# A four-mixer network on one core: beginning one output projection with its attention half, and splitting two mixers' weights ahead of time

## The chip, the cores and the metric

The kernel runs on one core of a Trainium2 chip. The metric is the device time of one execution in microseconds (us); less is better. In the traces PE is TensorE, DVE is VectorE, ACT is ScalarE, POOL is GpSimd and SP is SyncE, which here only issues transfers.

## What is computed

A sequence of 512 tokens with 1024 channels, in float32, goes through six stages. Each is a sandwich: normalize, transform, normalize, add to the input.

```python
# block one: h = rms_norm(x, pre); x = x + rms_norm(mixer(h), post)
E1: even_mixer    retention + stick-breaking attention, concatenated, @ w_out
O1: odd_mixer     gated linear recurrence + LRU, concatenated, @ w_out
# block two: x = x + rmsnorm(fn(rmsnorm(x, g_pre)), g_post)
def even_mixer_2(t, ...):                       # E2, the third mixer
    proj = t @ w_in
    y_a = diff_attention(proj[..., :3 * DIFF_WIDTH], ...)   # 4 heads, 512 channels out
    y_b = conformer_conv(proj[..., 3 * DIFF_WIDTH:], ...)   # gated 31-tap causal conv, layernorm, silu
    return jnp.concatenate([y_a, y_b], axis=-1) @ w_out
F0: swiglu(t, w_gate, w_up, w_down)             # hidden width 2816
O2: odd_mixer_2   s5_ssm (256 channels) + mla_attention (6 heads), concatenated, @ w_out
F1: swiglu
```

In `diff_attention` each head's output is the difference of two softmax attentions, and the 128 channels of each head are then divided by their root mean square. In `conformer_conv` the 512 convolved channels of a token go through one layernorm, so that its statistics need all 31 taps of all four channel tiles.

## The kernel before

Tokens lie in four blocks of 128 (`NB = 4`); matrices are cut into 128x128 tiles. To keep float32 accuracy, every large product is made of three matmuls (`mm3`): each operand is split into a high part `h` (a rounded copy) and a low part `l = x - h`, and h·h, h·l and l·h are summed in PSUM. So every weight piece of 128x1024 values has to be split before TensorE can use it. `wload` does that: SP loads the raw piece into one of three `wr` buffers, ACT copies it to `wh` (line 132), DVE subtracts to get `wl` (line 115). `wh` and `wl` have five buffers each. For an output projection some pieces go to larger `wb` tiles (`big=True`), which come from the pool of 14 tiles of 4x512 that also holds activations (`A4`).

`projT` projects with the channels on the partitions, one piece per 128 output channels. `projS` projects with the tokens on the partitions: its four pieces are all needed for each of the four token blocks, so all four stay in their buffers until the last block.

`outp` is the output projection and the two normalizations behind it. The input channels come as pieces in the order `order`. The first `nK - tail` pieces are multiplied into all four token blocks; then, block by block, the last `tail` pieces, so that a block can be normalized while the next is multiplied. Its sums lie in all eight PSUM banks (PP, ZZ, ZO, WW for the four blocks).

The third mixer, `even2`, first projects the convolution's two halves (`e2t`); the 4 x 30 taps (`taps`, line 750, on DVE) have the low priority `prio(-1500)`, so DVE does them when nothing else is ready. Then q, k and v are projected, and four heads go through `scores` (scores, softmax of two score matrices, difference, transposes) and `av_` (times v). The end of the stage, and the order of the output projection, are:

```python
        scores(3)
        av_(1)
        av_(2)
        stats()      # transpose ycv (PE), sums and squares (ACT): needs all taps
        av_(3)
        norm()       # layernorm: rstd and scaling (DVE)
        silu()       # transpose back (PE), Silu (ACT), split: channels 512..1023
        heads()      # over_rms (DVE), transpose (PE), split: channels 0..511
        self.order = [4, 5, 6, 7, 0, 1, 2, 3]
```

The instructions are placed on the five engines' queues when the kernel is built: among those that are ready by the planner's own estimate of times, the one with the highest priority is next (by default program order; `prio(1200)` puts one 1200 instructions further up). On the chip each queue then runs strictly in that order, and waits at its head. Buffers, PSUM banks included, are given out in the same planning, when the first instruction that writes one is placed.

Of the kernel before, what the change touches and what calls it, by code (L numbers as in the profile page):

```python
# [8 lines left out]
F32 = mybir.dt.float32  # L9
F32R = mybir.dt.float32r  # L10
# [7 lines left out]
P = 128  # L18
S = 512
NB = 4  # L20
# [30 lines left out]
class Net:  # L51
    def __init__(self, ctx, tc, A, out):
        self.tc, self.nc, self.A, self.out = tc, tc.nc, A, out
        pool = lambda name, **k: ctx.enter_context(tc.tile_pool(name=name, **k))
        self.cst_p = pool("cst", bufs=1)
        self.w_p = pool("w", bufs=5)
        self.a_p = pool("a", bufs=14)
        self.u_p = pool("u", bufs=13)
        self.s_p = pool("s", bufs=40)
        self.ps = pool("ps", bufs=1, space=PSUM)  # L60
        self.d_p = pool("dram", bufs=1, space=bass.MemoryType.DRAM)

        self.banks = {"P": 2, "Z": 3, "W": 2, "O": 1}
        self.xdram = [self.d_p.tile([P, NB, 2, 512], F32, name=f"xd{i}") for i in range(2)]
        self.xn = 0
        self.gates = []
        self.n = 0
        nc = self.nc
        self.cst = self.cst_p.tile([P, C_N], F32, name="cst")
        nc.gpsimd.dma_start(self.cst[:, :P], A["cst"][:, :P])  # L70
        self.vec = self.cst_p.tile([P, V_N], F32, name="vec")
        self.ident = self.cst[:, C_ID : C_ID + P]
        self.xsrc = A["x"].rearrange("(b p) d -> p b d", p=P)
        self.k = self.cst_p.tile([P, 8], F32, name="k")
        for i, v in enumerate((EPS, 0.0, 1.0, HALF_PI)):
            nc.vector.memset(self.k[:, i : i + 1], v)
        with self.prio(9000):
            nc.scalar.activation(self.k[:, 5:6], self.k[:, 2:3], AF.Sqrt)
        self.ones = self.cst_p.tile([P, P], F32, name="ones")
        nc.vector.memset(self.ones, 1.0)  # L80
        self.eps, self.zero, self.one, self.hpi = (self.k[:, i : i + 1] for i in range(4))
# [36 lines left out]
        self.nc.scalar.copy(h, src)  # L118
        self.lo(l, src, h)

    def wload(self, name, i, cols, big=False, pool=False):
        nc = self.nc
        with self.prio(1200):
            raw = self.w_p.tile([P, 1024], F32, tag="wr", bufs=3, name=self.nm("wr"))[:, :cols]
            nc.sync.dma_start(raw, self.A[name][i])
            if big:
                h, l = (t.rearrange("p a d -> p (a d)") for t in (lambda w: (w[:, 0:2], w[:, 2:4]))(self.A4(F32R, "wb")))
            else:
                h = self.w_p.tile([P, 1024], F32R, tag="wh", name=self.nm("wh"))[:, :cols]
                l = self.w_p.tile([P, 1024], F32R, tag="wl", name=self.nm("wl"))[:, :cols]  # L130
        with self.prio(9000 if self.gates else 1200):
            c = nc.scalar.copy(h, raw)  # L132
            if pool:
                s = nc.gpsimd.tensor_tensor(l, raw, h.bitcast(F32), ALU.subtract)
            else:
                s = self.lo(l, raw, h)
        if self.gates:
            for r, g in zip((c, s), self.gates.pop(0)):
                self.hold(r, g)
        return h, l  # L140

    def mm3(self, out, a, b, first, last, hold=None):
# [129 lines left out]
    def xb(self, b):  # L272
        return self.x[b // 2][:, 2 * (b % 2) : 2 * (b % 2) + 2]

    def outp(self, name, order, lhs, post, pre, tail=7, last=False, nbig=4, in_turn=False):

        nc = self.nc
        yb = [[self.bank(t, "y") for t in tags] for tags in ("PP", "ZZ", "ZO", "WW")]
        nK = len(order)
        gate = max(0, nK - tail - 3)  # L280
        first = []
# [2 lines left out]
        def mm(n, w, b):  # L284
            k = order[n]
            h, l = lhs(k)
            sl = slice(b * P, b * P + P)
            for j in range(2):
# [2 lines left out]
                prev[b] = r  # L291
                if n == gate and not first:
                    first.append(r)

        for n in range(nK - tail):
            w = self.wload(name, order[n], 1024)
            for b in range(NB):
                mm(n, w, b)
        ws = [self.wload(name, order[n], 1024, big=n - nK + tail < nbig) for n in range(nK - tail, nK)]
        with self.prio(100):  # L300
            self.load_x(first[0])
# [8 lines left out]
        for b in range(NB):  # L310
            if in_turn and b > 1:
                held[b, 0] = held[b, 1] = prev[b - 1]
            for n in range(nK - tail, nK):
                mm(n, ws[n - nK + tail], b)
            with self.prio(6000):
# [15 lines left out]
                    self.prenorm(b, prew)  # L331
            if not last:
                nc.scalar.dma_start(dst[:, b], self.xb(b))
        if not last:
            self.xsrc = dst.rearrange("p b a d -> p b (a d)")

# [376 lines left out]
    def even2(self):  # L713
        nc = self.nc
# [134 lines left out]
        scores(3)  # L849
        av_(1)  # L850
        av_(2)
        stats()
        av_(3)
        norm()
        silu()
        heads()
        self.order = [4, 5, 6, 7, 0, 1, 2, 3]


    def exp_tiny(self, dst, x, t, n):  # L860
# [349 lines left out]
def net(ctx, tc, A, out, phases="E1 O1 E2 F0 O2 F1"):  # L1210
    n = Net(ctx, tc, A, out)
    ph = phases.split()
# [4 lines left out]
        n.s5_setup()  # L1217
    for i, p in enumerate(ph):
        lhs = n.mix
        if p == "E1":  # L1220
            n.even1()
        elif p == "O1":
# [5 lines left out]
        else:  # L1228
            n.ffn(p.lower() + "gu")
            lhs = n.lhs  # L1230
            if p == "F0" and "O2" in ph:
                n.s5_setup()
        last = i == len(ph) - 1
        n.outp(wout[p], n.order, lhs, 6 + pres[p], None if last else pres[ph[i + 1]], last=last, in_turn=p == "O2")

# [154 lines left out]
```

## Time and profile before

| | |
|---|---|
| median of three runs | 1719.47 us (1714.02 to 1721.96) |
| the profiled execution, whole | 1708.09 us |
| the profiled execution, first to last instruction (span) | 1706.3 us |
| TensorE busy | 1657.1 us, 97% of the span |
| VectorE busy | 964.3 us, 57% |
| ScalarE busy | 669.6 us, 39% |
| mean granted TensorE clock | 0.987 |

Read it so: TensorE is busy nearly all the time, so what a change can win lies in the few stretches where it is not, or where its clock is granted below 1. All times inside the trace count from the start of the span. E1 takes about the first 241 us with its output projection, O1 goes to about 530, E2 to 759, F0 to 1127, O2 to about 1340 and F1 to the end.

### The profile page before, as it was taken

What the parts mean: (1) busy time and instruction counts of PE and PEld (TensorE: products, weight loads), DVE (VectorE), ACT (ScalarE), POOL (GpSimd) and SP (SyncE); (2) the same over time, 40 slices, a digit from 0 to 9 for tenths busy, and PEclk for the clock granted to TensorE, in tenths of its full rate; (3) what the DMA queues carried; (4) which work ended last, traced back from release to release, by engine and by line L of the source; (5) the groups of instructions that cost most, each with busy time, mean ns of one, the idle gap of its engine ahead of it and who ended that gap; (6) DMA issues with size and microseconds to landing.
All of it is one profiled execution on the core that took longest, in us unless ns stands there. A gap on an engine that the chain in (4) does not pass through costs nothing. (4 is left out here: it accounts for less than half of the span.)

```text
span 1706.3 us, 20536 instructions
## 1 busy us (share of the span) xinstructions
PE 1657.1 (97%) x8008; PEld 1318.5 (77%) x8008; DVE 964.3 (57%) x1824; ACT 669.6 (39%) x1174; POOL 2.0 (0%) x8
## 2 busy tenths in 40 slices
PE   8999999999999998699999999999999999999998
PEld 8657788988789875588888888886447988888886
DVE  7564456765676998763222278468695622224332
ACT  5554234214545246543222244344456422224231
POOL 0000000000000000000000000000000000000000
PEclk8999999999999999799999999999999999999999
DMA  5212243202153220152223235432005323222341
GB/s 204 84 38 74 80 179 117 72 29 99 62 198 115 74 84 1 65 195 101 98 99 99 99 118 196 170 126 78 25 25 197 112 99 99 99 98 89 97 161 50
DMA packets 50241, 175.06 MB, mean 103 GB/s; under 512 B 5584, under 2 KB 6096, under 8 KB 50016
## 3 DMA queue, kind: packets, MB, share of 16 engines
q1 hardware_dynamic: 40896, 142.20, 24.6%
q10 hardware_dynamic: 9216, 31.48, 4.9%
q8 instruction: 63, 1.03, 0.3%
q14 instruction: 34, 0.28, 0.1%
q0 software_dynamic: 32, 0.07, 0.0%
HBM read 156.95 MB, written 16.78 MB: 102 GB/s over the span
## 5 line engine op out<-in xcount | busy, mean ns | idle before, releaser
L115 DVE TENSOR_TENSOR wl<-wr,wh 128x1024 fp32r<-128x1024 f32 (+2 forms) x224 | 271.3, 1213 | 350.4 <-ACT wh L132 335.4
L132 ACT CAST wh<-wr 128x1024 fp32r<-128x1024 f32 (+2 forms) x224 | 233.0, 1042 | 534.8 <-PE pp L147 409.8
L147 PE MATMUL pp<-xl,wh 128*128 128x512 f32 (+1 forms) x1184 | 428.1, 362 | 0.2 <-DVE xl L115 0.2
L144 PE MATMUL pp<-xh,wh 128*128 128x512 f32 (+1 forms) x1184 | 425.2, 361 | 1.2 <-ACT xh L234 1.2
L148 PE MATMUL pp<-xh,wl 128*128 128x512 f32 (+1 forms) x1184 | 425.3, 360 | 0.0
L144 PEld LDWEIGHTS pp<-xh,wh 128*128 128x128 f32 x1184 | 223.6, 190 | 36.1 <-ACT xh L234 2.5
L147 PEld LDWEIGHTS pp<-xl,wh 128*128 128x128 f32 x1184 | 224.4, 190 | 34.0 <-DVE xl L115 1.2
L148 PEld LDWEIGHTS pp<-xh,wl 128*128 128x128 f32 x1184 | 224.4, 190 | 33.7 <-issue 2.3
L147 PE MATMUL pp<-wl,xh 128*128 128x512 f32 (+1 forms) x320 | 126.9, 396 | 0.0
L148 PE MATMUL pp<-wh,xl 128*128 128x512 f32 (+1 forms) x320 | 125.9, 394 | 0.0
L144 PE MATMUL pp<-wh,xh 128*128 128x512 f32 (+1 forms) x320 | 125.9, 393 | 0.0
L144 PE MATMUL y<-wh,ah 128*128 128x512 f32 x288 | 112.5, 390 | 0.0
L147 PE MATMUL y<-wl,ah 128*128 128x512 f32 x288 | 112.3, 390 | 0.0
L148 PE MATMUL y<-wh,al 128*128 128x512 f32 x288 | 112.2, 389 | 0.0
L1189 DVE TENSOR_TENSOR act<-g,pp 128x512 f32<-128x512 f32 x44 | 30.2, 687 | 132.9 <-PE pp L148 131.5
L750 DVE SCALAR_TENSOR_TENSOR ycv<-up,vec,ycv 128x512 f32<-128x512 f32 x120 | 84.4, 740 | 0.4
L144 PEld LDWEIGHTS pp<-wh,xh 128*128 128x128 f32 x320 | 60.2, 188 | 13.9 <-issue 2.6
L147 PEld LDWEIGHTS pp<-wl,xh 128*128 128x128 f32 x320 | 60.2, 188 | 12.9 <-issue 2.4
L148 PEld LDWEIGHTS pp<-wh,xl 128*128 128x128 f32 x320 | 60.3, 188 | 11.1 <-issue 0.6
L321 DVE TENSOR_TENSOR yn<-y,nw 128x512 f32<-128x512 f32 x48 | 31.8, 685 | 58.0 <-ACT yn L319 52.2
L144 PEld LDWEIGHTS y<-wh,ah 128*128 128x128 f32 x288 | 54.1, 188 | 11.5 <-issue 0.4
L148 PEld LDWEIGHTS y<-wh,al 128*128 128x128 f32 x288 | 54.1, 188 | 11.1
(373 smaller groups left out, 2314.0 us busy)
## 6 DMA issues: line engine op xcount, KB each, us to landing
wr<-in_f0gu SPq DMA_DIRECT2D x44, 512.0 KB, 3.3
wr<-in_f1gu SPq DMA_DIRECT2D x44, 512.0 KB, 3.3
wr<-in_f0d SPq DMA_DIRECT2D x22, 512.0 KB, 3.4
wr<-in_f1d SPq DMA_DIRECT2D x22, 512.0 KB, 3.3
xd<-x ACTq DMA_DIRECT2D x20, 512.0 KB, 2.7
x<-xd ACTq DMA_DIRECT2D x20, 512.0 KB, 6.7
wr<-in_o1t SPq DMA_DIRECT2D x16, 512.0 KB, 3.3
nw<-in_nw ACTq DMA_DIRECT2D x12, 512.0 KB, 9.5
```

Source lines behind the costliest of these rows:

```text
L115: return self.nc.vector.tensor_tensor(l, src, h.bitcast(F32), ALU.subtract)
L132: c = nc.scalar.copy(h, raw)
L144: r = mm(out, lhsT=a[0], rhs=b[0], start=first, stop=False)
L147: mm(out, lhsT=a[0], rhs=b[1], start=False, stop=False)
L148: return mm(out, lhsT=a[1], rhs=b[0], start=False, stop=last)
L321: nc.vector.tensor_tensor(yn[j], yb[b][j], postw[j], ALU.mult)
L750: V.scalar_tensor_tensor(y, up[:, j : j + 512], self.v("dw", 4 * j + t), y, ALU.mult, ALU.add)
L1189: nc.vector.tensor_tensor(act[k // 4][:, k % 4], g, ps, ALU.mult)
```

## The change

Two edits in the same step.

1. In E2 the order of the output projection becomes 0 to 7, attention half first, and `stats`, `norm` and `silu` are handed to `outp` as `mid`. `outp` now has `tail=4`: it multiplies the four attention pieces into token blocks 0, 1 and 2, then issues `mid`, then goes on block by block with the four convolution pieces; block 3, whose two banks (WW) `mid` uses for its transposes, gets its attention pieces just before its convolution pieces.
2. During E1 and O1, at every second weight load outside an output projection, one piece of E2's weights is loaded and split (`keep_ahead`), and both halves are stored to DRAM by two transfers from POOL's queue. E1 and O1 have 52 such loads, so 26 of E2's 28 pieces are kept (all but the last two of `e2out`). During F0, with 44 loads, all 19 listed pieces of O2 are kept in the same way (all O2 weights but `o2glu`). When E2 and O2 ask for a kept piece, `wload` loads its two halves straight into `wh` and `wl` (or `wb`), with two transfers from SP and no work for ACT or DVE.

```diff
-    def wload(self, name, i, cols, big=False, pool=False):
-        nc = self.nc
+    def plan(self, pieces, every):
+
+        self.ahead, self.every, self.nw = pieces, every, 0
+
+    def keep_ahead(self):
+        nc = self.nc
+        name, i, cols = self.ahead.pop(0)
+        t = self.d_p.tile([P, 2, cols], F32, name=f"kp_{name}_{i}")
+        for j, s in enumerate(self.wload(name, i, cols, keep=True)):
+            nc.gpsimd.dma_start(t[:, j], s.bitcast(F32))
+        self.kept[name, i] = t
+
+    def wload(self, name, i, cols, big=False, pool=False, keep=False):
+        nc = self.nc
+        if (name, i) in self.kept:
+            t = self.kept[name, i]
+            with self.prio(1200):
+                if big:
+                    h, l = (t.rearrange("p a d -> p (a d)") for t in (lambda w: (w[:, 0:2], w[:, 2:4]))(self.A4(F32R, "wb")))
+                else:
+                    h = self.w_p.tile([P, 1024], F32R, tag="wh", name=self.nm("wh"))[:, :cols]
+                    l = self.w_p.tile([P, 1024], F32R, tag="wl", name=self.nm("wl"))[:, :cols]
+                nc.sync.dma_start(h.bitcast(F32), t[:, 0])
+                nc.sync.dma_start(l.bitcast(F32), t[:, 1])
+            return h, l
...
+        if self.ahead and not keep:
+            self.nw += 1
+            if self.nw % self.every == 0:
+                self.keep_ahead()
         return h, l
...
-    def outp(self, name, order, lhs, post, pre, tail=7, last=False, nbig=4, in_turn=False):
+    def outp(self, name, order, lhs, post, pre, tail=7, last=False, nbig=4, in_turn=False, mid=None):
...
+        ahead, self.ahead = self.ahead, []
...
+        early = []
 
         for n in range(nK - tail):
-            w = self.wload(name, order[n], 1024)
-            for b in range(NB):
-                mm(n, w, b)
+            early.append(self.wload(name, order[n], 1024))
+            for b in range(NB - 1 if mid else NB):
+                mm(n, early[n], b)
+        if mid:
+            mid()
...
+            if mid and b == NB - 1:
+                for n in range(nK - tail):
+                    mm(n, early[n], b)
             for n in range(nK - tail, nK):
                 mm(n, ws[n - nK + tail], b)
...
+        self.ahead = ahead
...
         av_(1)
         av_(2)
-        stats()
         av_(3)
-        norm()
-        silu()
         heads()
-        self.order = [4, 5, 6, 7, 0, 1, 2, 3]
+        self.order = list(range(8))
+
+        def mid():
+            stats()
+            norm()
+            silu()
+
+        self.mid = mid
...
+        if p == "E1" and "E2" in ph:
+            n.plan([("e2t", i, 1024) for i in range(8)] + [(f"e2{z}", i, 1024) for z in "qkv" for i in range(4)]
+                   + [("e2out", i, 1024) for i in range(8)], 2)
+        if p == "F0" and "O2" in ph:
+            n.plan([("o2t", i, 1024) for i in range(2)] + [("o2s", i, 896) for i in range(4)]
+                   + [("o2kv", 0, 768), ("o2q", 0, 768), ("o2q", 1, 768), ("o2q", 2, 768), ("o2kv", 1, 768)]
+                   + [("o2out", i, 1024) for i in (2, 3, 4, 5, 6, 7, 0, 1)], 2)
...
+        n.outp(wout[p], n.order, lhs, 6 + pres[p], None if last else pres[ph[i + 1]], last=last, in_turn=p == "O2",
+               **(dict(tail=4, mid=n.mid) if p == "E2" else {}))
```

## Rows read from the trace of the kernel before

**Rows 1.** The page's busy times: us, share of the span, instructions.

```profile
PE 1657.1 (97%) x8008; PEld 1318.5 (77%) x8008; DVE 964.3 (57%) x1824; ACT 669.6 (39%) x1174; POOL 2.0 (0%) x8
```

**Rows 2.** By stage: length; PE, PEld, DVE, ACT, POOL busy; clock; DMA share; GB/s.

```profile
0.00:488.00 488.00, 478.52 (x2512) 383.26 (x2513) 299.88 (x692) 208.07 (x357) 1.39 (x7) 0.99 0.27 95
548.00:621.00 73.00, 73.00 (x345) 59.28 (x344) 72.82 (x125) 23.64 (x31) 0.00 (x0) 1.00 0.26 87
621.00:655.50 34.50, 34.31 (x145) 22.62 (x145) 30.11 (x91) 20.27 (x54) 0.00 (x0) 1.00 0.13 46
655.50:688.40 32.90, 27.45 (x140) 18.57 (x138) 27.72 (x85) 19.60 (x56) 0.00 (x0) 0.90 0.00 1
688.40:708.80 20.40, 6.20 (x26) 4.63 (x27) 14.22 (x44) 9.94 (x24) 0.00 (x0) 0.55 0.00 0
708.80:759.20 50.40, 48.65 (x226) 39.97 (x225) 31.33 (x46) 27.44 (x48) 0.00 (x0) 0.98 0.49 178
860.00:880.00 20.00, 20.00 (x90) 16.57 (x89) 6.28 (x6) 5.20 (x6) 0.00 (x0) 1.00 0.27 94
1170.00:1290.00 120.00, 113.81 (x393) 57.79 (x393) 97.94 (x206) 61.71 (x143) 0.00 (x0) 0.99 0.11 37
```

**Rows 3.** The hole in slices of 3 us, same columns.

```profile
689.00:692.00 3.00, 0.00 (x0) 0.00 (x0) 2.89 (x5) 0.42 (x1) 0.00 (x0) 0.77 0.00 0
698.00:701.00 3.00, 1.11 (x6) 0.71 (x4) 0.31 (x2) 3.00 (x11) 0.00 (x0) 0.50 0.00 0
713.00:716.00 3.00, 3.00 (x19) 2.53 (x18) 2.82 (x4) 3.00 (x4) 0.00 (x0) 1.00 0.00 0
```

**Rows 4.** The convolution's tile ycv alone: PE, PEld, DVE busy by stretch.

```profile
548.00:621.00 73.00, 0.00 (x0) 0.00 (x0) 52.22 (x77) 1.00 0.26 87
621.00:696.00 75.00, 1.77 (x7) 1.27 (x8) 33.80 (x47) 0.92 0.06 22
```

**Rows 5.** Weight splits: line 115 in three stretches, then line 132's group.

```profile
L115 DVE TENSOR_TENSOR wl<-wr,wh x13: 1215/1218/1224, 549.1 to 619.8; 128x1024 fp32r<-128x1024 f32 x13
...
L115 DVE TENSOR_TENSOR wl<-wr,wh x1: 1209/1209/1209, 622.7 to 622.7; 128x1024 fp32r<-128x1024 f32 x1
...
L115 DVE TENSOR_TENSOR wl<-wr,wh x10: 684/959/1225, 1128.8 to 1184.1; 128x768 fp32r<-128x768 f32 x5, 128x896 fp32r<-128x896 f32 x3, 128x512 fp32r<-128x512 f32 x1, 128x1024 fp32r<-128x1024 f32 x1
...
L132 ACT CAST wh<-wr 128x1024 fp32r<-128x1024 f32 (+2 forms) x224 | 233.0, 1042 | 534.8 <-PE pp L147 409.8
```

**Rows 6.** Timeline 688 to 712: start, duration, work, count, idle before and releaser.

```profile
688.35 0.60 ACT L369 ACTIVATE sq<-po 128x512 f32<-128x512 f32 x1 [1.80 <-PE po L359]
...
688.98 0.69 DVE L371 TENSOR_REDUCE hs<-sq 128x4 f32<-128x512 f32 x1 [1.84 <-ACT sq L369]
689.58 6.25 DVE L750 SCALAR_TENSOR_TENSOR ycv<-up,vec,ycv 128x512 f32<-128x512 f32 x8
...
695.89 0.69 PE L202 MATMUL pt<-cst,ycv 128*128 128x128 f32 x2 [7.58 <-DVE ycv L750]
...
702.15 0.17 DVE L193 TENSOR_SCALAR h<-hs 128x16 f32<-128x16 f32 x1
...
705.94 0.17 DVE L198 SCALAR_TENSOR_TENSOR r<-t,r 128x16 f32<-128x16 f32 x1
706.15 2.50 DVE L382 TENSOR_TENSOR on<-on,r 128x512 f32<-128x512 f32 x4
...
708.85 0.78 PE L144 MATMUL y<-wh,mh 128*128 128x512 f32 x1
...
711.99 1.37 ACT L841 ACTIVATE mh<-pt,lqt 128x512 fp32r<-128x512 f32 x2 [0.74 <-PE pt L202]
```

**Rows 7.** Transfers: issues with KB and us to landing; DMA at 731 to 734.

```profile
xd<-x ACTq DMA_DIRECT2D x20, 512.0 KB, 2.7
...
cst<-in_cst POOLq DMA_DIRECT2D x1, 64.0 KB, 6.3
...
731.00:734.00 3.00, 3.00 (x15) 2.49 (x14) 0.00 (x0) 2.38 (x4) 0.00 (x0) 1.00 1.02 410
```

More of the change, by code (lines that the diff above doesn't have):

```diff
@@ L66, in __init__ @@
         self.gates = []
+        self.kept, self.ahead, self.every, self.nw = {}, [], 0, 0
         self.n = 0
@@ L1233, in net @@
         last = i == len(ph) - 1
-        n.outp(wout[p], n.order, lhs, 6 + pres[p], None if last else pres[ph[i + 1]], last=last, in_turn=p == "O2")
+        n.outp(wout[p], n.order, lhs, 6 + pres[p], None if last else pres[ph[i + 1]], last=last, in_turn=p == "O2",
+               **(dict(tail=4, mid=n.mid) if p == "E2" else {}))
 def _tables(np):
```

## The prediction

> **What bounds the kernel now.** I read the busy times first: TensorE is busy 97% of the span, 1657.1 of 1706.3 us [rows 1]. So only about 49 us can be won at all, plus what is lost to a low clock, and the question is where these lie. The second view, busy time by stage, answers that [rows 2]. Of the first 488 us (E1 and O1) TensorE is idle 9.5. In F0 it is full, 90 matmuls in 20 us, which gives 0.222 us per matmul of 512 columns at full clock. The largest loss is the end of E2. From 655.5 to 688.4 it idles 5.45 us at a mean clock of 0.90, from 688.4 to 708.8 it works only 6.2 of 20.4 us, at 0.55. Together that is 19.65 us of idling. The third view cuts this hole into slices [rows 3]: nothing runs from 689 to 692, the clock is 0.50 from 698 to 701 (1.2 GHz of 2.4), and back at 1.00 by 713.
>
> The fourth view, the timeline [rows 6], says why. At 688.98 the last head is reduced; then DVE has eight taps left, and TensorE waits 7.58 us for them, until 695.89. What follows is a chain over three engines: statistics, layernorm, transposes, Silu, split. It lets the first matmul of the output projection start at 708.85. The attention heads, whose sums of squares were ready at 689.7, wait behind that: their own normalization begins at 702.15, because the convolution half comes first.
>
> Why are the taps late? DVE is busy 72.82 of 73.00 us from 548 to 621 [rows 2]. In that stretch it made 77 taps (52.22 us) [rows 4] and 13 weight splits of 1.22 us [rows 5]; 47 taps were left for the attention, where DVE is again busy 30.11 of 34.5 and 27.72 of 32.9 us. So in E2 every weight split pushes taps back, and the last tap sets the end. That is unlike the rest of the program, where TensorE is the bound.
>
> **Part one: splits leave E2.** Thirteen splits before 621 and one just after leave DVE: 14 x 1.22 = 17.1 us. A tap costs 52.22/77 = 0.68 us while DVE does little else, so 25 more taps fit before 623 or so, and 22 of the 47 remain. DVE has them to do in the 67 us of attention in which it did 39, so I expect the last tap near 660, not at 695.8. Then statistics, layernorm and Silu of the convolution (16 + 16 transposes, 16 ACT instructions) can run in gaps of the attention or just behind it. Their 28 us of cover is what hides them; with the taps still late they cost the chain of now, 695.9 to 708.8, which part two covers.
>
> With some 15 us of taps (22 x 0.68) gone from the stretch 655.5 to 688.4, softmax steps wait less for DVE. At most its idle time and half of what its clock lost can come back, 5.45 + 1.6 = 7 us; the least is nothing, since the statistics move in. I take 3: the last head ends near 685.4.
>
> **Part two: attention half first.** What now precedes the first matmul of the projection is the heads' chain. Its links have rows [rows 6]: square 0.60 and reduction up to 689.67, so 1.3 from 688.35; the 16-wide reciprocal root from 702.15 to 706.11, of which 1.9 belongs to layernorm scaling between, so 2.1; scaling 2.50; transposes and ACT's rounded copy of one head, 1.4 (0.69 of it ACT). That is 7.3, and the first matmul starts near 692.8 instead of 708.85: **16 us earlier**. TensorE is idle meanwhile but for transposes, so I count the low clock at the start of the projection once again, as it is now (0.55 before, 1.00 only by 713 [rows 2, 3]), and keep its whole length of 50.4 us. Inside it, 3 blocks x 4 pieces x 2 x 3 = 72 matmuls, 16 us at 0.222, run before the first convolution piece is needed. So even with the last tap at 695.8 the 13 us chain behind it is nearly covered: the two parts win the same hole, not two.
>
> Block 3 now has 48 matmuls at the end, 10.7 us, blocks 0 to 2 have 24, 5.3 us each, where each had 42; DVE needs some 6 us for a block's normalizations, and can catch up during block 3. Cost: 0, with -2 to +3 in the range.
>
> **Part three: loading instead of splitting in E2 and O2.** A kept piece is 1 MB instead of 0.5, and its transfer can begin only when a `wh` buffer is free, where before the raw piece was waiting in `wr` and needed 1.04 + 1.22 us. At the 410 GB/s of the busiest slice [rows 7] a piece takes 2.6 us. Between q, k and v four pieces follow four that free their buffers in steps of 1.3 us (6 matmuls), so the third and fourth come about 1 us late each time. I take 1.5 us in all; nothing if scores fill the gap, 5 at most. SP's queue holds only loads, so behind a waiting one stand the next pieces and no computation.
>
> In O2, 9 of 10 splits between 1126 and 1184 leave DVE, about 9 us [rows 5], as do 4 to 8 of `o2out` at its end. From 1170 to 1290 TensorE idles 6.2 of 120 us and is otherwise in float32 matmuls [rows 2]: it is nearly the bound, so I take 3 us of gain, with bounds 0 and 9.
>
> **Part four: what is added.** E1 and O1 get 26 splits: 27 us of ACT, 32 of DVE, against 280 and 188 us of idle time there [rows 2]. F0 gets 19, with DVE at 6.28 of 20. 45 pieces are stored by 90 transfers of at most 0.5 MB and read back. In F0 two loads, one more load and two stores per 11 us make 2.6 MB, 240 GB/s, under the 410 seen. The cover is TensorE's own stream; I take 2 us, mostly at the crowded start and in E1's attention.
>
> **The sum.** -16 + 1.5 - 3 + 2 = -15.5. The profiled execution takes 1708.09 us, 1.8 more than its span, so it would take 1692.6, 0.9% less. The median of the runs shown is 1719.47, 0.67% above that execution; the same share off gives 1704.
>
> **Rivals.** *The stores hold the buffers.* Each kept piece occupies one of five `wh` and `wl` buffers until its stores land, and ACT and DVE run in order: a split for a buffer not yet free blocks softmax, evacuation and all else behind it. For: POOL's one transfer took 6.3 us for 64 KB, while a store of 512 KB from ACT's queue took 2.7 [rows 7]; E1 and O1 hold four pieces at a time in seven projections. Against: a group of four lasts 22 us, long enough for a store of 6, and DVE is 61% busy there. The rival cancels the gain at 17.5/26 = 0.7 us of TensorE idle per kept piece in E1 and O1; at 1.2 us it gives +13, 1732 scaled. The Trainium skill, SBUF — State Buffer, section "SBUF: two separate sides", says that a transfer from POOL's queue cannot get its descriptors while DVE runs certain instructions that take both port pairs, so that it looks blocked. By that rule the landing grows with DVE's load; no row here has such a store under a busy DVE.
>
> *The hole only changes its owner.* The heads' chain leaves TensorE idle as the taps did; if the last head still ends at 688.4, DVE mixes taps into the chain (1 tap per link, 5 x 0.68), and loads come late by 5, the gain is 15.5 - 3 - 3.4 - 3.5 - 1 = 4.6 us: 1715, within half a percent, which is about what a measurement of this kernel can tell from no change. For it speaks that the planner placed taps between softmax steps before.
>
> *O2 gives as much as it could.* With 9 us there instead of 3, and 4 more from the attention of E2, it is -25.5: 1694. For it: DVE is at 82% from 1170 to 1290; against: TensorE at 95%.
>
> *The splits leave, yet DVE ends as late*, if taps keep their late places. Then only the reordering works, first matmul near 697 with taps mixed in, and about 10 us are won: 1709.
>
> **How the numbers follow.** Forecast (1704) 0.45, taps late (1709) 0.12, O2 in full (1694) 0.13, changed owner (1715) 0.17, stores (1732) 0.13. Faster by over 0.5% (below 1710.9): most of the first three, 0.66; within: 0.20; slower by over 0.5%: 0.14. The range from 1692 to 1723 leaves out most of the stores' rival and the best of O2; the likeliest case alone has 1698 to 1710.
>
> **What would show it.** Part one: the last tap before 670, no split by line 115 between 548 and 620. Part two: the first matmul of the third output projection near 693, some 7 us behind the last head, and the projection's end near 743 instead of 759. Part three: TensorE waits of about 1 us on loads of `wh` between q, k and v. Part four: E1 and O1 end within 2 us of now. Wrong would be: the start of E2 later by more than 5 us, ACT or DVE waiting on POOL's stores, or idle time of more than 10 us left between the last head and the projection.

## The result: 3% slower, and the profile after

The changed kernel takes 1773.91 us (median of 4 runs, 1767.66 to 1778.81) against 1720.72 us of the kernel before beside it (1714.02 to 1728.97): a ratio of 1.0305, 95% interval 1.0248 to 1.0362. The forecast was 1704 us. The profiled execution of the changed kernel spans 1776.6 us, 70.3 more than the one before.

Busy times of the page, to be read against [rows 1]:

```profile
PE 1691.9 (95%) x8008; PEld 1335.9 (75%) x8008; DVE 966.5 (54%) x1824; ACT 670.3 (38%) x1174; POOL 50.6 (3%) x98
```

TensorE executes as many matmuls as before, is busy 34.8 us longer and idle 35.5 us longer. So half of the loss is waiting, and half is the same work at a lower clock (a mean of 0.969 instead of 0.987). The profiled execution of before (1708.09 us) is shorter than all four timed beside the change, and that of the changed kernel (1778.81) is the longest of its four. So what is 70.3 us between the two profiles is 53.2 us between the medians, and the differences by stage below are 17 us too large in all.

The stages, cut in each trace at the start of the first and the end of the last matmul of each output projection (us; before, E1 ends at 289.7 with its projection, and the 241 given ahead of the prediction is about the end of its mixer):

| stage | before | after | difference |
|---|---|---|---|
| E1 mixer, projection | 242.6, 47.1 | 268.4, 47.0 | +25.7, 0 |
| O1 mixer, projection | 182.5, 52.0 | 202.4, 57.3 | +19.9, +5.3 |
| E2 mixer, projection | 184.6, 50.6 | 170.4, 62.1 | -14.3, +11.5 |
| F0 mixer, projection | 244.1, 123.6 | 258.4, 123.7 | +14.4, 0 |
| O2 mixer, projection | 152.1, 57.3 | 160.8, 58.3 | +8.7, +1.1 |
| F1 to the end | 369.8 | 367.8 | -2.0 |

E2's mixer gives most of what was hoped for. E1 and O1, which only prepare it, lose 51 us; E2's projection and F0's mixer lose 26.

**Where E1 and O1 lose.** Busy times by stretch (columns as in [rows 2]): E1's and O1's mixers of the changed kernel, then of the kernel before.

```profile
0.00:268.35 268.35, 245.23 (x1168) 182.40 (x1169) 156.65 (x392) 126.91 (x221) 16.36 (x35) 0.94 0.50 169
...
315.38:517.77 202.39, 188.16 (x1057) 158.79 (x1056) 129.61 (x259) 79.01 (x114) 12.18 (x22) 0.97 0.46 158
```

```profile
0.00:242.60 242.60, 233.37 (x1168) 176.83 (x1169) 140.04 (x378) 112.81 (x207) 1.39 (x7) 0.98 0.28 97
...
289.70:472.20 182.50, 182.31 (x1056) 154.90 (x1056) 121.02 (x257) 67.06 (x102) 0.00 (x0) 1.00 0.21 74
```

In E1 TensorE idles 23.1 us instead of 9.2, and the same 1168 matmuls take 11.9 us longer at a mean clock of 0.94 instead of 0.98. DVE gets 17 us of work and ACT 14 and both stay far from full, so neither has become the bound. What they do is wait. The view of waits of the changed kernel, 0 to 575 us (sum, times, longest), first ACT and then DVE:

```profile
ACT wh L157 <- DMA kp_e2v<-wh: 10.5, 2, 6.1
ACT wh L157 <- DMA kp_e2t<-wh: 6.2, 2, 4.1
```

```profile
DVE wl L117 <- DMA kp_e2out<-wl: 11.1, 4, 3.8
DVE wl L117 <- DMA kp_e2k<-wl: 9.5, 2, 6.1
DVE wl L117 <- DMA kp_e2t<-wl: 9.1, 2, 6.3
```

With the groups not shown, ACT stands 30.4 us and DVE 38.2 us in front of a split (lines 157 and 117, formerly 132 and 115), because the buffer it is to fill is still being stored. The timeline shows what one such wait does (five answers: POOL, DVE, SP, ACT, PE):

```profile
31.20 0.53 POOL L132 DMA_DIRECT2D kp_e2t<-wl  x1 [0.73 <-DVE lqt L756]
...
37.74 1.22 DVE L117 TENSOR_TENSOR wl<-wr,wh 128x1024 fp32r<-128x1024 f32 x1 [2.81 <-DMA kp_e2t<-wl]
...
39.00 2.46 SPq L150 DMA_DIRECT2D wr<-in_e1sv  x2
...
43.13 1.05 ACT L157 CAST wh<-wr 128x1024 fp32r<-128x1024 f32 x1 [4.02 <-DMA wr<-in_e1sv]
...
47.37 0.76 PE L176 MATMUL pp<-wl,xh 128*128 128x512 f32 x1 [2.63 <-DVE wl L117]
```

DVE has split a kept piece, and POOL issues the store of its low half at 31.20. The very next split on DVE is given the same buffer: it stands at the head of the queue from 34.93, 3.7 us behind the issue, and waits 2.81 us more for the landing. This split frees a raw buffer only at 38.96, so SP issues the next load of E1's own weights at 39.00; ACT waits 4.02 us for that piece, its low half is begun at 46.09, and TensorE idles 2.63 us. That loads wait for splits is nothing new (50 of SP's loads did so up to 524 us of before, 66 up to 575 us here); what is new is that the splits wait for stores, and a late split is a late load. This is the one place where TensorE's idle time ends with a weight split itself. The rest of its 41.8 us up to the end of O1 (9.6 before) ends with other work of DVE and ACT, whose queues hold the waiting splits; that each of these gaps goes back to a held buffer is argued, not followed one by one.

**Where E2 and F0 lose.** The timeline of the changed kernel around the third projection, which answers to [rows 6]:

```profile
738.56 0.69 DVE L409 TENSOR_REDUCE hs<-sq 128x4 f32<-128x512 f32 x1 [3.83 <-ACT sq L407]
...
742.49 2.41 PE L231 MATMUL pt<-cst,on 128*128 128x128 f32 x8 [4.60 <-DVE on L420]
745.46 0.80 PE L173 MATMUL y<-wh,mh 128*128 128x512 f32 x1 [0.56 <-ACT mh L879]
...
765.20 1.03 PE L231 MATMUL pt<-cst,ycv 128*128 128x128 f32 x8
...
773.96 1.97 PE L231 MATMUL pt<-cst,yS 128*128 128x128 f32 x8 [6.15 <-DVE yS L859]
...
778.96 0.79 PE L173 MATMUL y<-wh,mh 128*128 128x512 f32 x1 [0.41 <-ACT m L868]
```

The last head is reduced at 739.25 and the first matmul follows 6.2 us later. But the convolution's transposes start only at 765.20, behind all 72 early matmuls, although its last tap was done at 709.2:

```profile
L788 DVE SCALAR_TENSOR_TENSOR ycv<-up,vec,ycv x120: 673/745/753, 597.3 to 708.5; 128x512 f32<-128x512 f32 x120
```

From 765.2 to 779.0 TensorE works at the convolution's chain and idles in it. And behind the projection the normalization runs late. ACT stores each normalized block (`xd<-x`): before at 739.94, 746.58, 759.46 and

```profile
768.03 0.33 ACTq L333 DMA_DIRECT2D xd<-x  x1
```

which is 8.6 us behind the last matmul of the projection (759.42); after, at 805.79, 815.12, 822.57 and

```profile
831.82 0.33 ACTq L370 DMA_DIRECT2D xd<-x  x1
```

24.3 us behind it (807.57). F0's projections need these blocks, and F0 is 14.4 us longer. Of these, some 11 come with the new order alone (a_reorder below) and 3 to 4 with the kept pieces alone (b_keep).

### The profile page after: what moved, and what is told of

It is laid out like the page before. It is cut to its first block, busy times and chain, and to the rows that moved or that the text cites. A ratio compares the mean times of both kernels' runs of the same rounds, so it can differ in the third digit from the quotient of the medians.

```text
span 1776.6 us, 20924 instructions
## 1 busy us (share of the span) xinstructions
PE 1691.9 (95%) x8008; PEld 1335.9 (75%) x8008; DVE 966.5 (54%) x1824; ACT 670.3 (38%) x1174; POOL 50.6 (3%) x98
## 3 DMA queue, kind: packets, MB, share of 16 engines
q8 instruction: 63, 1.03, 0.2%
## 4 chain that ended last, share of the span: by engine, by line
PE 51%; issue 42%; DVE 2%; DMA 2%; POOL 2%; ACT 2%; SPq 0%; ACTq 0%; POOLq 0%; DVEq 0%
PE pp L173 10%; PE pp L176 10%; PE pp L177 10%; PE y L173 5%; PE y L177 5%; PE y L176 5%; PE sc L1166 1%; PE sc L1165 1%; PE pt L231 1%; PE po L1180 1%; PE py L1085 1%; PE pw L231 1%; PE py L1086 1%; DMA x<-in_x 0%; DVE wl L117 0%
## 5 line engine op out<-in xcount | busy, mean ns | idle before, releaser
L117 DVE TENSOR_TENSOR wl<-wr,wh 128x1024 fp32r<-128x1024 f32 (+2 forms) x230 | 278.3, 1213 | 406.2 <-ACT wh L157 277.5
L157 ACT CAST wh<-wr 128x1024 fp32r<-128x1024 f32 (+2 forms) x230 | 238.2, 1043 | 519.8 <-PE pp L176 270.4
L173 PEld LDWEIGHTS pp<-xh,wh 128*128 128x128 f32 x1184 | 225.5, 191 | 35.9 <-ACT xh L263 2.3
L177 PEld LDWEIGHTS y<-wh,al 128*128 128x128 f32 x288 | 54.1, 188 | 11.3
```

What stands on the lines that cost most here:

```text
L117: return self.nc.vector.tensor_tensor(l, src, h.bitcast(F32), ALU.subtract)
L173: r = mm(out, lhsT=a[0], rhs=b[0], start=first, stop=False)
L177: return mm(out, lhsT=a[1], rhs=b[0], start=False, stop=last)
```

## The experiments

All runs in one table: ratio to the kernel before with its interval; then, from each profile, the end of O1's projection, E2's mixer and projection, F0's mixer, and all of O2 (us). There is one profile of each.

| run | ratio (95%) | O1 ends | E2 | F0 mixer | O2 |
|---|---|---|---|---|---|
| before | 1 | 524.2 | 184.6 + 50.6 | 244.1 | 209.3 |
| changed | 1.0305 (1.0248-1.0362) | 575.1 | 170.4 + 62.1 | 258.4 | 219.1 |
| a_reorder | 1.0142 (1.0093-1.0191) | 523.7 | 182.6 + 64.6 | 255.4 | 218.0 |
| b_keep | 1.0208 (1.0149-1.0268) | 590.2 | 172.5 + 49.5 | 248.0 | 212.1 |
| c_split_only | 1.0103 (1.0056-1.0150) | 528.5 | 191.6 + 50.3 | 247.4 | 224.6 |
| d_store_only | 1.0430 (1.0366-1.0495) | 577.0 | 199.3 + 50.9 | 251.2 | 219.5 |
| e_sp_store | 1.0189 (1.0130-1.0248) | 535.5 | 197.6 + 50.1 | 249.6 | 214.8 |
| f_big | 1.0170 (1.0112-1.0228) | 541.7 | 188.2 + 52.0 | 244.7 | 223.1 |
| n1_tiny | 1.0179 (1.0127-1.0231) | 538.6 | 196.8 + 49.5 | 248.4 | 226.7 |
| n2_act_store | 1.0318 (1.0276-1.0361) | 561.2 | 197.3 + 51.9 | 244.3 | 224.9 |
| n4_after_sp | 1.0114 (1.0070-1.0158) | 538.2 | 174.0 + 62.5 | 258.7 | 214.3 |
| g_conv_early | 1.0263 (1.0211-1.0314) | 573.0 | 185.6 + 48.9 | 247.3 | 215.0 |
| k_mid_prio | 1.0248 (1.0204-1.0292) | 580.1 | 170.5 + 52.8 | 256.0 | 212.1 |
| n3_loads_first | 1.0280 (1.0230-1.0330) | 574.4 | 169.9 + 60.1 | 255.2 | 214.7 |
| h_best | 1.0077 (1.0033-1.0122) | 544.2 | 184.8 + 49.1 | 242.3 | 214.6 |
| m_pool | 1.0141 (1.0084-1.0197) | 526.9 | 209.0 + 51.9 | 244.1 | 228.9 |
| i_keep20_sp | 0.9960 (0.9925-0.9996) | 530.0 | 173.3 + 48.5 | 244.1 | 217.8 |
| l_stats_P | 0.9958 (0.9922-0.9993) | 529.3 | 174.6 + 51.1 | 244.1 | 225.5 |

### Each edit alone

a_reorder keeps nothing; b_keep has the old end of `even2` and no `mid`.

```diff
 if p == "E1" and "E2" in ph:      # a_reorder: both plans off
-    n.plan(...)
 heads()                           # b_keep: stats, norm and silu back in place
-self.order = list(range(8))
+self.order = [4, 5, 6, 7, 0, 1, 2, 3]
```

> The first edit alone: attention half first, nothing kept. E1, O1, F0 and O2 should be as before, so all that differs lies from 525 to 800 us. Theory: DVE still makes 14 weight splits in E2, so the last tap stays late (near 690), but the heads no longer wait for it: the projection's first matmul comes near 697 instead of 708.9 (-12); inside the projection TensorE then waits for the layernorm chain and at the end for the next stage's normalization, as in the changed kernel, +11 in the projection and +9 behind it. Sum +8 or less, a ratio of 1.000 to 1.006. Rival: with the taps this late the layernorm chain is hidden no better and the loss is above 10 us, 1.008 or more. If the ratio is below 0.996, the reordering was a gain that the second edit ate.

> The second edit alone: all 45 pieces kept, the third projection in its old order. Theory (keeping is the loss): E1 and O1 together +51 us as in the changed kernel, F0 +4, O2 +9, E2's mixer shorter by 14 or more, its projection 50: a ratio of 1.025 to 1.035. Rival (the reordering is most of the loss): 1.015 or less.

Neither edit pays alone. The reordering costs 1.4%: the rival's size. The last tap is late (705.7) and DVE now puts one tap of 0.75 us behind each link of the heads' reciprocal root, eleven of them, so that the first matmul comes at 706.3 instead of 708.9: 2.5 us are won, not 12. The projection then takes 64.6 us and F0's mixer 255.4. Keeping costs 2.1%, less than expected: E1 and O1 lose 66 us in its profile, but with the old order E2 takes 222.0 us instead of 235.2, better than in the changed kernel (232.5).

The 66 us are no larger price than the 51. Up to the end of O1 the two kernels have nearly the same instructions in the same order, and TensorE idles 41.8 us in the changed kernel and 42.4 in b_keep (length less PE busy); what differs is the granted clock (first the changed kernel, then b_keep):

```profile
0.00:575.11 575.11, 533.29 (x2679) 423.44 (x2679) 348.29 (x750) 248.31 (x413) 29.60 (x59) 0.96 0.48 166
```

```profile
0.00:590.17 590.17, 547.81 (x2679) 436.27 (x2679) 348.70 (x750) 248.62 (x413) 29.62 (x59) 0.93 0.47 162
```

All six kernels here with whole stores from POOL's queue out of `wh` and `wl` idle 40.7 to 42.9 us up to there, at a clock of 0.93 to 0.97, and end between 573.0 and 590.2. So the idle time, some 32 us more than before, comes back in every profile; the rest of the loss, 18 to 33 us in which the same matmuls take longer at a lower clock, differs between executions.

### Splits, stores and held buffers

c_split_only and d_store_only are built on the kernel before, with the plans. In both the pieces are never used; the last two of E2's 28 fall into E2 itself, which may be part of why its mixer is longer here.

```diff
 for j, s in enumerate(self.wload(name, i, cols, keep=True)):
-    nc.gpsimd.dma_start(t[:, j], s.bitcast(F32))   # c_split_only: no store
-self.kept[name, i] = t                             # c and d: E2 and O2 split their own
```

> Built on the kernel before, order of the projection unchanged: the 45 extra pieces are loaded and split in E1, O1 and F0, but never stored and never used; E2 and O2 load and split their weights themselves as before. Theory (the stores hold the wh and wl buffers): without stores a buffer is free as soon as it is split, so E1 and O1 lose little, 0.2 us per piece for ACT's and DVE's work, +5 us, F0 +2: a ratio of 1.002 to 1.008. Rival (the extra pieces do the harm by themselves, as they take wr, wh and wl buffers and places in ACT's and DVE's queues): E1 and O1 +40 or more as in the changed kernel, a ratio of 1.025 or more.

> As the run without stores, but with the 90 stores; the stored pieces are not read, E2 and O2 load and split their weights themselves as before. Theory (the stores hold the buffers): E1 and O1 +45 to +51, F0 +4 to +10, E2 and O2 as before, a ratio of 1.03 to 1.035. Rival (reading back is what costs): no more than the run without stores, 1.01 or less. The difference to the run without stores is the price of the stores.

This separates them: E1 and O1 end 4.3 us later with 26 more loads and splits, 52.8 us later with their stores as well. Reading back costs nothing that shows: b_keep, which reads the pieces, has the lower ratio. d_store_only's 1.0430 lies above the expected 1.03 to 1.035; beside E1 and O1, E2 is 15 and O2 10 us longer in its profile. The ratio of c_split_only lies above its expected 1.002 to 1.008, and most of its profile's excess lies in E2 (7 us) and in O2 (15 us), whose code is unchanged (see the end).

Then the stores were varied: issued from SP (e_sp_store) or from ACT (n2_act_store), made from `wb` tiles that no next weight needs (f_big), or cut to 8 columns of each piece (n1_tiny); n4_after_sp is the changed kernel with SP's queue.

```diff
-nc.gpsimd.dma_start(t[:, j], s.bitcast(F32))
+nc.sync.dma_start(t[:, j], s.bitcast(F32))             # e_sp_store, n4_after_sp
+nc.scalar.dma_start(t[:, j], s.bitcast(F32))           # n2_act_store
+nc.gpsimd.dma_start(t[:, j, :8], s[:, :8].bitcast(F32))  # n1_tiny
-self.wload(name, i, cols, keep=True)
+self.wload(name, i, cols, big=True, keep=True)         # f_big
```

> As the run that stores and does not use (1.043), but the 90 stores go out from SP's queue instead of POOL's. E1 and O1 with their projections took 524 us before, 529 with splits alone, 577 with POOL's stores. Theory (a buffer is held for as long as its store takes, whoever issues it, and ACT and DVE wait in order for it): the landing is a little shorter from SP, but SP's queue now stands at each store until the split is done and holds the weight loads behind it; E1 and O1 still 555 to 585, a ratio of 1.03 to 1.05. Rival (POOL's way of issuing is what makes the stores slow, its landing of 3.4 to 7.1 us under a busy DVE): E1 and O1 back to 529 to 540, a ratio of 1.01 to 1.018.

> As the run that stores and does not use (1.043), stores from POOL, but the extra pieces are split into wb tiles of the pool of 14 instead of wh and wl. Nothing that the stages need next is written over a piece that is still being stored, unless the pool of 14 runs short. Theory (held wh and wl buffers are the price of the stores): no split of a wh or wl waits for a store, E1 and O1 end at 529 to 540 instead of 577, a ratio of 1.010 to 1.018. Rival (the traffic and POOL's issues cost by themselves, 63 MB more than before or so): E1 and O1 stay above 560, a ratio of 1.03 or more. If the pool of 14 is short, waits move to its tiles (x, mh, wt): between the two.

> As the run that stores and does not use (stores from POOL, 1.043; E1 and O1 with projections 577 us against 529 with splits alone), but each of the 90 stores takes only the first 8 of up to 1024 columns. POOL issues as many transfers at the same places; the bytes and with them the landing shrink. Theory (a wh or wl is held until its store lands, and 4 to 6 us of that are the bytes): E1 and O1 end between 532 and 550. Rival (what costs is POOL itself: its issues, its waits, or the planner's places for them): E1 and O1 still end above 565, as they would with whole stores.

> As the run that stores and does not use, but with the 90 whole stores issued from ACT's queue. With SP's queue E1 and O1 ended at 535.5, with POOL's at 577, though both landed in 3.4 to 6.5 us. Rival (any queue but POOL's is cheap): 530 to 545. Theory (the price hangs on which instructions stand behind a store or behind a split that waits for one, and ACT's own queue is full of what TensorE needs): 550 or more, since ACT now stands at each store until DVE has made the low half.

> The changed kernel with one word changed: the stores go out from SP's queue instead of POOL's. If what the runs without use showed holds in the changed kernel: E1 and O1 end at 535 to 545 instead of 575, the rest as in the changed kernel: 30 to 40 us less than 1773.9, a ratio of 1.008 to 1.014. Rival (there the stores were cheap only because nothing read them back): 1.02 or more.

The time that ACT and DVE stand in front of a buffer being stored, up to the end of O1, summed from the view of waits:

| run | ACT | DVE | O1 ends |
|---|---|---|---|
| c_split_only | 0 | 0 | 528.5 |
| f_big | 0 | 0 | 541.7 |
| n1_tiny | 16.8 | 12.4 | 538.6 |
| e_sp_store | 21.3 | 16.5 | 535.5 |
| n4_after_sp | 25.2 | 19.9 | 538.2 |
| n2_act_store | 17.1 | 29.8 | 561.2 |
| d_store_only | 26.9 | 33.2 | 577.0 |
| changed | 30.4 | 38.2 | 575.1 |

With the same POOL stores from other buffers the waits are gone and so are 35 of the 48 us. What is left in f_big lies in part elsewhere: in O1's projection TensorE idles 4.1 us for pieces in `wb` tiles, whose raw pieces are loaded late. Short stores of as many issues give back 38 us. So POOL's issuing is not the price, and the rival of n1_tiny falls. But the theory of e_sp_store falls, too: it was held that the queue makes no difference. There whole stores hold the same buffers, and E1 and O1 lose only 7 us more than with splits alone; in n4_after_sp, the changed kernel with SP's queue, 10 instead of 47, as its theory said. So a held buffer is not yet a loss; it becomes one where a split asks for it too soon. Nor is any queue but POOL's cheap: from ACT's the loss is 33, and the rival of n2_act_store falls. Issues of E2's q pieces, d_store_only and then e_sp_store (KB, median us to landing):

```profile
kp_e2q<-wh POOLq DMA_DIRECT2D x4, 512.0 KB, 3.5
kp_e2q<-wl POOLq DMA_DIRECT2D x4, 512.0 KB, 5.3
```

```profile
kp_e2q<-wh SPq DMA_DIRECT2D x4, 512.0 KB, 3.6
kp_e2q<-wl SPq DMA_DIRECT2D x4, 512.0 KB, 5.0
```

The stores land nearly as fast from POOL as from SP: the medians of the five groups of pieces (e2t, q, k, v, e2out) differ by 0.8 us at most, in either direction. The Trainium skill, SBUF — State Buffer, section "SBUF: two separate sides", says that a transfer from POOL's queue waits for its descriptors while DVE runs an operation in a mode that also takes the pair of SBUF ports it shares with GpSimd, and that one from ACT's or SP's queue does not. Of these two remedies SP's queue gave back 41 of the 48 us and ACT's 16, and no trace here shows the reason that the Trainium skill names. What differs is how long DVE stands, 16.5 or 33.2 us, and the loss goes with that and not with ACT's waits: below 21 us of it E1 and O1 lose 7 to 10 us on top of the splits, at 30 us 33, above that 47. Each of these variants (another queue, another size, other buffers) also has another order of instructions on DVE and ACT, since the planner works with its own times for a store and places it in the queue that issues it; d_store_only and the changed kernel share one order, e_sp_store and n4_after_sp another. So what f_big and n1_tiny give back is not put down to buffers or bytes alone. That the order sets how soon a split asks for a held buffer can be read from the splits that wait: in d_store_only they reach the head of their queue 3.7 us (DVE, 12 splits) and 0.9 us (ACT, 8) behind the issue of the store that they wait for, on average, in e_sp_store 4.5 us (10) and 2.6 us (10). Why the planner's order with SP's queue comes out so well stays open.

### The late chain and the late blocks

g_conv_early has `stats`, `norm` and `silu` with `prio(2000)` behind `av_(1)` and no `mid`; k_mid_prio keeps `mid` and raises it; n3_loads_first also asks for the loads of x and the norm weights ahead of it.

```diff
 av_(1)                         # g_conv_early
+with self.prio(2000):
+    stats(); norm(); silu()
 if mid:                        # k_mid_prio
-    mid()
+    with self.prio(4000):
+        mid()
```

> The changed kernel, but the layernorm and Silu of the convolution are asked for with high priority inside the attention, and the projection goes its usual way (attention half first, one piece over all blocks and seven block by block). E1 and O1 as in the changed kernel (575). Theory (in the changed kernel this chain stood behind 72 matmuls that were placed before it, and its price is the projection's 62 us and most of F0's 14): the projection's first matmul some 6 to 8 us behind the last head, its length 50 to 53, F0 within 4 of before; 20 us less than the changed kernel, a ratio of 1.015 to 1.021 to the kernel before. Rival (the chain takes DVE and TensorE time from the attention that is as long as what it frees, or the taps are late): E2's mixer longer by 8 or more than the changed kernel's 170, ratio above 1.025.

> The changed kernel with one difference: the convolution's statistics, layernorm and Silu, asked for inside the projection, get a high priority, so that their transposes are not placed behind the 72 early matmuls. Theory (the 20 us of matmuls ahead of the chain are what exposes it): the third projection lasts 50 to 54 us instead of 62.1, TensorE no longer idles 6 us inside it, and F0 gives back part of its 14; 15 to 22 us less than the changed kernel's 1773.9, a ratio of 1.016 to 1.023. Rival (24 matmuls per block are too few to hide a block's normalization behind them, whatever the chain does): the projection gets shorter, but the idle time in front of F0's first matmuls stays near 9 us, and F0's mixer stays near 258 us, ratio 1.023 to 1.028.

> As the changed kernel with the convolution's chain at high priority (1760.5 us, 1.0248), and the loads of x and of the two norm weights are asked for before that chain, too. There DVE waited 8.6 us for the norm weights in front of the first block's normalization, and TensorE idled 7.4 us in F0's first 25. Theory (they are late only because they stand behind the chain in ACT's queue and in the giving out of the tiles): they are issued some 15 us earlier, the wait goes and F0's mixer is shorter by 5 to 8 of its 256 us, a ratio of 1.019 to 1.022. Rival (three tiles of the pool of 14 are simply not free before ycv and yS are done): issued as late as before, no difference.

In g_conv_early the projection is back at 48.9 us and F0 at 247.3, as the theory said, but E2's mixer is 15.2 us longer, as the rival said: mixer and projection together take 234.5 us, against 232.5 in the changed kernel. The transposes came 18 us behind the last tap (732.7 against 714.2), so the chain still ran at the end of the attention and behind it. In k_mid_prio the projection takes 52.8 us: the 72 matmuls ahead of the chain did cost 9 us. But F0 hardly moves (256.0), as its rival said. n3_loads_first shows that the late norm weights are not the reason: they are issued 5 us behind the projection's first matmul instead of 23 as in k_mid_prio, DVE no longer waits for them, yet F0 takes 255.2 us (and the chain, which comes behind them, is late again, so the projection is back at 60.1). Its normalized blocks are stored at

```profile
794.92 0.33 ACTq L375 DMA_DIRECT2D xd<-x  x1
804.69 0.33 ACTq L375 DMA_DIRECT2D xd<-x  x1
814.39 0.33 ACTq L375 DMA_DIRECT2D xd<-x  x1
824.17 0.33 ACTq L375 DMA_DIRECT2D xd<-x  x1
```

every 9.8 us, though their matmuls are done faster: here a block's chain over ACT and DVE takes that long, with F0's first splits between its links. In the changed kernel the steps are 9.3, 7.4 and 9.3 us. 42 matmuls of 0.222 us are 9.3 us, so in the old order a block can be normalized under the next; 24 are 5.3 us, and the blocks queue up. The last one is normalized 19.7 us behind the projection here, 20.4 in k_mid_prio, 21.2 in a_reorder and 24.3 in the changed kernel, 8.6 before; F0's mixer is longer by 11.1, 11.9, 11.3 and 14.4 us.

### Can it pay?

h_best joins g_conv_early and f_big without a plan for F0. i_keep20_sp keeps only what paid: 20 pieces (e2t, q, k, v), stored from SP, the old order, no plan for F0. l_stats_P gives the statistics' transposes the P banks. m_pool keeps nothing and makes the subtraction of those 20 splits on POOL (`pool=True` in `even2`).

```diff
-    + [("e2out", i, 1024) for i in range(8)], 2)     # i_keep20_sp, l_stats_P
-    n.plan([("o2t", i, 1024) ...                     # these two and h_best
-pt = self.bank("W", "pt")                            # l_stats_P, in stats
+pt = self.bank("P", "pt")
-self.projS("e2q", 512, rqk(0))                       # m_pool, and so for e2t, k, v
+self.projS("e2q", 512, rqk(0), pool=15)
```

> Both mends at once, and no pieces kept in F0: 26 pieces of E2 kept during E1 and O1 in wb tiles, convolution's chain inside the attention, usual projection with the attention half first. Theory: E1 and O1 +5 to +15, E2 mixer 170 and projection 51 instead of 185 and 51 (-14), F0, O2, F1 as before: 0.995 to 1.002. Rival (wb tiles do not free the splits of their waits): 1.015 or more. Whether the change can pay at all is settled here: below 0.995 it can.

> What is left of the change if only what paid is kept: the 20 pieces of e2t, q, k and v are kept during E1 and O1 (the 8 of the projection are not, and nothing in F0), stores from SP's queue, the convolution half first as before. Theory: E1 and O1 +6 to +10 (with 26 pieces and SP's stores it was +11), E2 shorter by 12 or 13 as in the run of the second edit alone (222 us instead of 235), the rest as before: -2 to -7 us, a ratio of 0.996 to 0.999. Rival: E1 and O1 eat it, 1.003 or more.

> As the run with 20 kept pieces, but the transposes for the convolution's statistics go to two PSUM banks (P) that the attention's softmax does not use for its own transposes, and have a high priority. Theory (in the run that asked for the chain early, the transposes began 19 us behind the last tap because the two W banks were taken): they begin within 6 us of the last tap, TensorE idles 5 us or more less in front of the projection, a ratio 0.003 below the run with 20 kept pieces. Rival (they are placed by the planner's own, later time of the last tap): no difference.

> The kernel before with one difference: the subtraction of the 20 weight splits of e2t, q, k and v is made by POOL instead of DVE; nothing is kept, nothing reordered. It takes 20 x 1.22 = 24 us from DVE in E2 without any store or read back. Theory (DVE's load in E2 sets the last tap, and that the end): E2 (235 us) shorter by 8 to 14, a ratio of 0.992 to 0.996. Rival (POOL's subtraction takes several times DVE's 1.2 us, and the projections wait for it, or both engines slow each other): E2's projections longer, a ratio of 1.005 or more.

h_best is slower than the kernel before: E1 and O1 lose 20 us, and E2, with the chain inside the attention, gains 1. i_keep20_sp is a little faster than the kernel before: 1716.32 against 1722.12 us beside it, 0.9960 (0.9925 to 0.9996), an interval that nearly reaches 1, with O1's end at +5.8 and E2 at -13.4, as expected. l_stats_P, with the same pieces kept, has the same ratio; it starts its transposes 22 us earlier and wins nothing by it. m_pool is slower. DVE's taps and POOL's subtractions at the same time:

```profile
612.52 13.18 DVE L750 SCALAR_TENSOR_TENSOR ycv<-up,vec,ycv 128x512 f32<-128x512 f32 x7
```

```profile
612.74 11.09 POOL L134 TENSOR_TENSOR wl<-wr,wh 128x1024 fp32r<-128x1024 f32 x4 [30.04 <-ACT wh L132]
```

Seven taps take 13.18 us beside four subtractions. One by one, three of them take 0.73 to 0.74 us as always and four 2.82 to 2.89, about as long as one subtraction (2.78 to 2.85): beside each subtraction one tap is held up. The same section of the Trainium skill says that a DVE operation with two inputs in SBUF and a GpSimd operation that reads SBUF exclude each other for a whole instruction; the trace agrees. That this is all of m_pool's loss was not tested.

## Why the prediction was wrong

**The step that failed is part four**, "I take 2 us" for what is added. It measured 51 us in E1 and O1, 2.0 us per kept piece, and 3 to 4 us in F0. Its cover, "TensorE's own stream", was judged by busy shares (DVE at 61%), but a split that waits for a buffer is not busy: it stops the queue behind it. The mechanism stood among the rivals, *The stores hold the buffers*, at 0.13, and its reason against (22 us for a group of four, long enough for a store of 6) failed on when a buffer is asked for again. The kept pieces come between the stage's own and use the same five buffers, and in the changed kernel DVE's waiting splits want theirs 3.8 us behind the issue of the store on average (13 splits, seven of them the very next split), while those stores take 5.1 to 8.9 us to land. The rival's price was 1.2 us of TensorE idle per piece, and that is what was measured: of the 51 us TensorE idles 32, which is 1.24 per piece. As no row stood behind the 1.2, the agreement is in part luck. What the rival left out are the 19 us of a lower clock, and the 26 of E2's projection and F0.

**A second term was mis-sized, in part two**: "DVE needs some 6 us for a block's normalizations ... Cost: 0, with -2 to +3". A block takes 7 to 10 us of ACT and DVE in turn, and with 24 matmuls per block that shows: 11 us in F0's mixer with the new order alone. And the 13 us chain of the convolution was not covered by the early matmuls but placed behind them: another 9 (62.1 us of projection against 52.8 in k_mid_prio).

**What was right.** Part one: the last tap ends 134.1 us behind O1's projection instead of 171.6, which is 658 in the times of before (forecast near 660). Part two's chain: the first matmul comes 7.5 us behind the start of the last head's squares (forecast 7.3), which is 6.2 behind its reduction. E2's mixer is 14.3 us shorter where 16 were counted: the chain gave the 13 forecast, the attention 1 instead of 3. Part three: TensorE waits 1.5 us for loads of kept pieces between q, k and v, as forecast, all of it in front of k. O2's 3 us came, too, but as idle time, and the clock hides them: O2 of before, then of the changed kernel,

```profile
1127.12:1336.46 209.34, 199.00 (x820) 127.15 (x820) 156.84 (x311) 103.28 (x234) 0.00 (x0) 0.99 0.26 89
```

```profile
1189.66:1408.78 219.12, 212.01 (x828) 131.54 (x828) 142.49 (x300) 93.05 (x224) 0.00 (x0) 0.93 0.34 121
```

TensorE idles 10.3 us in the one and 7.1 in the other, while the stage is 9.8 us longer at a mean granted clock of 0.93 instead of 0.99. The six profiles with O2's pieces kept idle 7.1 to 8.7 us there, the twelve without 10.3 to 13.1. *The hole only changes its owner* did not happen with both edits, but a_reorder alone is just that, tap by tap.

## What to carry to other kernels

Spare time on DVE and ACT does not make work free when it is moved into a stage that TensorE fills: ask which buffers it holds, for how long, how soon one is asked for again, and what stands behind the instruction that next needs one, since a queue in order turns a late buffer into late loads. A reordering that cuts the pieces between two consumers must be held against the consumer's whole chain, links and hand-overs included, not against its busy time. And what is asked for late in program order is placed behind all that is ready, however long its inputs have been there.

## What the runs showed of the hardware

TensorE's clock differs between executions of unchanged work. Two stretches of O2, of the kernel before and of c_split_only, whose code there is the same:

```profile
1185.00:1205.00 20.00, 19.37 (x84) 12.81 (x82) 14.71 (x31) 6.27 (x14) 0.00 (x0) 1.00 0.17 53
1205.00:1225.00 20.00, 18.96 (x61) 8.93 (x60) 13.50 (x32) 11.67 (x30) 0.00 (x0) 0.95 0.10 33
```

```profile
1200.00:1220.00 20.00, 19.37 (x85) 12.96 (x84) 15.37 (x31) 6.27 (x14) 0.00 (x0) 1.00 0.17 53
1220.00:1240.00 20.00, 20.00 (x51) 9.36 (x50) 8.22 (x21) 8.98 (x23) 0.00 (x0) 0.74 0.08 26
```

Behind the same 20 us at full clock, the granted clock stays at 0.95 in the one and falls to 0.74 in the other, between the levels of 2.4 and 1.2 GHz, and the second gets through 51 matmuls instead of 61. In the twelve profiles with this code all of O2 took 209 to 229 us, the 209 in the kernel before. Executions of the kernel before show it, too: a span of 1710.0 us at a mean clock of 0.985 and of 1725.3 at 0.977, with a product of 1684 and 1686. Over the 46 executions beside the experiments the spans go from 1706.8 to 1731.5 us (1.4%) and the products from 1681 to 1694 (0.8%). So up to about a per cent of this kernel's time goes with a clock that no edit here decided, and single profiles of two kernels are better held against each other by TensorE's idle time than by the length of a stage.
